# A hybrid decoder layer on one core: small fp32 products of the token mixers moved into four column strips of the TensorE array

## Chip, cores and metric

One Trainium2 chip, one NeuronCore of it. The metric is the device time of one launch in microseconds (us); the median of three runs counts. The program is one decoder layer for 2048 tokens of width 1024.

## The reference

The layer has two groups of token mixers side by side, a sandwich of RMS norms, a squared-ReLU MLP and a gated per-layer embedding. What the change touches are the two mixers and the norm of their heads:

```python
# gated DeltaNet, 4 heads, chunks of 64: a triangular solve per chunk
a_mat = eye(c) + where(strict, einsum('bhncd,bhnsd->bhncs', k_beta, k) * decay, 0)
u = triangular_solve(a_mat, v_beta, lower, unit_diagonal)
w = triangular_solve(a_mat, k_beta * exp(gc)[..., None], lower, unit_diagonal)
...
# HGRN2, 4 heads, chunks of 16: per-channel decay between query i and key j
pair = exp(where(causal, b_n[:, :, None] - b_n[:, None, :], -inf))
att  = einsum('bihd,bjhd,bijhd->bhij', q_n, k_n, pair)
...
def gated_head_norm(o, w, z):
    return o * rsqrt(mean(o * o, -1) + EPS) * w * silu(z)
```

## The kernel before, in words

Everything is kept transposed, channels on the 128 partitions and tokens along the free dimension, in four blocks of 512 tokens (q = 0 to 3). The wide products (input projection `mm`, line 1139; output projection `mmo`, lines 1022 and 1171; MLP `u` and `d` and gate `mmg`, line 1171) split each fp32 operand into two fp32r parts and add three products of 128x128 weights with 512 columns.

While the input projections run, the mixers run in between. The loop from line 1125 goes over the `works`: one for the decays (`ab`) and 32 projections for each q. Each work has 24 matmuls and is cut into three ticks of eight; after each tick `tick()` (line 376), and in its middle `half()`, step those generators that the `agenda` has for that time. A pair of heads (one GDN, one HGRN) starts every 24 ticks. `A_STEPS` (line 56) lists the ticks of the steps of `gdn_mixer`, `B_STEPS` (line 60) those of `hgrn_mixer`; the last pair has tables of its own. So two numbers in a table decide which small matmuls stand together in TensorE's queue between two wide ones. TensorE's order is the order of the code (`manual_schedule`), SyncE's too within this loop.

Three kinds of small products matter here; all are plain fp32, on the full 128x128 array.

- **HGRN's levels** (`hgrn_mixer`, `LEVELS`): the attention of a 128-token chunk is built in doubling distances s = 1, 2, 4, ..., 64. The distances 1 and 2 come from one step (line 874: four products `at_h`, 128 keys by 128 queries), 4 to 64 from one step each (line 889: two products). The result is a PSUM bank of pool `pp`, and of each 128x128 product only the entries near the diagonal are kept: VectorE's masked copy (line 896) takes them into `att`.
- **The inverse of GDN's triangular matrix** (`gdn_mixer`): 32x32 blocks are inverted on VectorE (lines 733 and 735), then two doublings join them, each by two block products: `psp`, `psx` and `pst` from 32 to 64, `psp` and `psd` from 64 to 128. The helper `pairs` (line 753) multiplies whole 128x128 operands that are mostly zero blocks, two products each.
- **The heads' norms** (`norm_steps`, line 273, called by `finish`): the sum over 128 channels is a product with a matrix of ones. The squares are split into two fp32r parts `hl` (ScalarE line 172, VectorE line 173), two products of 512 columns are added (lines 279 and 280), row 0 of the result is copied (line 282), stored, and read back as 128x4 for the square root. The norm of the early embedding tiles (`nrm_e`) uses the same function.

PSUM has eight banks: `pm` 2, `pp` 4 (also called `ph`), `po` 2. Each small product takes the next of the four `pp` banks and waits until the reader of the tile four before is done.

Of the kernel before, what the change touches and what calls it, by code (L numbers as in the profile page):

```python
# [24 lines left out]
QT = 512  # L25
NQ = T // QT
NC = QT // P
# [4 lines left out]
SB = 32  # L32
NB = P // SB
# [63 lines left out]
def trunk(ctx, tc, x, xT, pT, vecs, w_in, w_ab, gdn_a_log, gdn_dt_bias, w_out, w_up, w_down,  # L97
          w_ple, w_gate, consts, out):
    nc = tc.nc
    V, S, G, PE = nc.vector, nc.scalar, nc.gpsimd, nc.tensor  # L100
# [10 lines left out]
    ph = pp  # L111
# [8 lines left out]
    mixers = ctx.enter_context(ExitStack())  # L120
    cm = mixers.enter_context(tc.tile_pool(name="cm", bufs=1))
    cst = cm.tile([P, N_CONST, P], F32, name="cst")
    rows = cp.tile([N_ROWS, P], F32, name="rows")
# [38 lines left out]
    ones = cp.tile([P, P], F32R, name="ones")  # L162
# [7 lines left out]
    def split(t, eng, raw):  # L170

        S.activation(t[:, 0], raw, AF.Copy)  # L172
        eng.tensor_tensor(t[:, 1], raw, t[:, 0], ALU.subtract)  # L173
# [98 lines left out]

    def norm_steps(acc, scale, eps, name, done, pool=None):

        hl = st.tile([P, 2, QT], F32R, tag="hl", name=f"hl_{name}", bufs=1)
        split(hl, V, acc)
        yield
        ps = bank(f"nrm_{name}", pool or pp)
        PE.matmul(ps, ones, hl[:, 0, :], start=True, stop=False)
# [4 lines left out]
        nc.sync.dma_start(sd, row)  # L284
# [172 lines left out]
    with mixers as mctx:  # L457
# [12 lines left out]
        um = {lev: mp.tile([P, NC // 2, P], F32, name=f"um{lev}") for lev in (5, 6)}  # L470
        part = {lev: mp.tile([P, NC // 2, P], F32, name=f"part{lev}") for lev in (5, 6)}
# [148 lines left out]
        halves = [slice(0, P // 2), slice(P // 2, P)]  # L620

        def rows_of(g):
            return slice(g * SB, (g + 1) * SB)

        def gdn_mixer(q, h, live):

            n = f"g{q}_{h}"
# [8 lines left out]
            both = sm.tile([P, 2, NC], F32, tag="tail", name=f"tail_{n}")  # L636
# [93 lines left out]
            for i in range(0, SB, 2):  # L730
                j = SB - 2 - i
# [16 lines left out]
            V.transpose(flat(xt), flat(xn))  # L748
            yield

            def pairs(out, lhsT, rhs):
                for p in range(2):
                    PE.matmul(out[:, p], lhsT[:, p], rhs[:, p], start=True, stop=True)

            def two(t):
                return t.rearrange("p (n two) i -> p n (two i)", two=2)
# [3 lines left out]

            def ends(t):
                return bass.AP(t.tensor, t.offset, [list(t.ap[0]), [P, 2], [3 * SB, 2], [1, SB]])
# [5 lines left out]
            pairs(psp, um[5], ends(xn))  # L770
# [5 lines left out]
            pairs(psx, two(xt), ends(part[5]))  # L776
            pairs(pst, part[5], two(xt)[:, :, SB : 3 * SB])
# [6 lines left out]
            pairs(psp, um[6], two(xn))  # L784
# [4 lines left out]
            pairs(psd, part[6], two(xt))  # L789
# [47 lines left out]
        def hgrn_mixer(q, h, live):  # L837
# [26 lines left out]
            for lev, s in enumerate(LEVELS):  # L864
# [3 lines left out]
                m = nb // 4  # L868
                if lev == 1:
                    ps0 = bank(f"at_{n}_d", ph)[:, : QT // 2]  # L870
                    PE.matmul(ps0, one, own, start=True, stop=True)
                    ps1 = bank(f"at_{n}_{lev}", ph).rearrange("p (c n) -> p c n", c=NC)
                    for c in range(NC):
                        PE.matmul(ps1[:, c, :], k[:, blk(c)], both[:, :, c * P // 2 : (c + 1) * P // 2],
                                  start=True, stop=True)
                    chunks = ps1.rearrange("p (a b) n -> p a b n", a=2)
                    eye = bass.AP(ident.tensor, ident.offset, [list(ident.ap[0]), [1, 2], [0, 2], [2, P // 2], [1, 1]])
                    V.tensor_tensor(side_of_chunks(columns_of, 1, False),
                                    ps0.rearrange("p (a b n s) -> p a b n s", a=2, b=2, s=1), eye, ALU.mult)
                    V.tensor_tensor(side_of_chunks(columns_of, 1, True), chunks[:, :, :, : P // 2, None],  # L880
                                    mask[0][:, None, None, :, None].broadcast_to([P, 2, 2, P // 2, 1]), ALU.mult)
                    ps = chunks[:, :, :, P // 2 :]
                else:

                    ps = bank(f"at_{n}_{lev}", ph)[:, : QT // 2].rearrange("p (a b n) -> p a b n", a=2, b=2)
                    for c in range(2):
                        queries = bass.AP(qq.tensor, qq.offset + c * P + s,
                                          [list(qq.ap[0]), [QT // 2 - s, 2], [2 * s, P // (2 * s)], [1, s]])
                        PE.matmul(ps[:, :, c, :], keys[:, blk(c)], queries, start=True, stop=True)  # L889
# [229 lines left out]
        with tc.manual_schedule(engines={mybir.EngineType.SP}):  # L1119
# [32 lines left out]
            outs.close()  # L1152
            nc.sync.dma_start(*held_y.pop())

    ctx.enter_context(tc.tile_pool(name="pad", bufs=1)).tile([P, 48], F32, name="pad")
    second.append(ctx.enter_context(tc.tile_pool(name="rb", bufs=18, reuse_waits="tile")))
    f2 = ctx.enter_context(tc.tile_pool(name="f2", bufs=1, reuse_waits="tile"))
# [788 lines left out]
```

## Time and profile before

| | us |
|---|---|
| median of three runs (lowest, highest) | 2665.27 (2663.72, 2666.59) |
| the profiled execution's own time | 2665.86 |
| its span, first to last instruction | 2664.1 |
| TensorE matmul busy | 2637.0 (99%) |
| VectorE busy | 1968.0 (74%) |
| ScalarE busy | 1468.8 (55%) |
| granted TensorE clock | 1.000 |

In rows of the trace, `128*128 128x512 f32` is the rows and columns of the array that an instruction uses, then the moving operand's partitions and elements. A plain fp32 product appears as two matmul records, each with a weight load of its own, an fp32r product as one; the two records of one fp32 product are called its two passes here. PE is the matmul, PEld the weight load. The end of a matmul is modelled with the time that its result takes through the array (0.275 us for 128 moving elements, 0.389 us for 512); successive matmuls overlap in it, so what a product costs is the distance of starts: for a row of n equal passes that lasts t, (t - end of one) / (n - 1).

### The profile page before, as it was taken

To read this page: it belongs to the slowest core of one execution; us is meant where nothing else is said; L and a number is where in the kernel's file an instruction comes from. 1 tells how busy PE (TensorE), PEld (TensorE's weight loads), DVE (VectorE), ACT (ScalarE), POOL (GpSimd) and SP (SyncE) were. 2 spreads that over 40 slices of the span, in tenths; PEclk is the share of its full clock that TensorE was granted. 3 is DMA by queue.
4 is the path that set the end of the run, shared out by engine and by line. 5 is a ranking of instruction groups with operands and counts; after the bars stand their busy time and mean duration, and the time that the engine had idled before them with its cause. 6 is when DMAs were issued, how large, how long until landed. Compare 5 with 4: busy or idle time off the path is not lost.

```text
span 2664.1 us, 38284 instructions
## 1 busy us (share of the span) xinstructions
PE 2637.0 (99%) x12745; PEld 2209.8 (83%) x12745; DVE 1968.0 (74%) x4029; ACT 1468.8 (55%) x2991; POOL 136.4 (5%) x147
## 2 busy tenths in 40 slices
PE   8999999999999999999999999999999999999999
PEld 6888888888888888877888888888888888888887
DVE  7778777786677677578988867767877765468775
ACT  6666555465455456566565555555554555565431
POOL 0000000000000000010000000001000001101000
PEclk9999999999999999999999999999999999999999
DMA  8787777667666775682766476666544465677663
GB/s 281 274 261 256 241 268 238 227 225 240 218 212 221 234 220 176 203 250 102 242 213 202 164 242 219 213 204 207 199 171 145 160 236 187 198 253 250 209 224 124
DMA packets 267766, 573.51 MB, mean 215 GB/s; under 512 B 55578, under 2 KB 60152, under 8 KB 250416
## 3 DMA queue, kind: packets, MB, share of 16 engines
q1 hardware_dynamic: 265264, 566.86, 63.9%
q0 software_dynamic: 2304, 4.20, 0.9%
q8 instruction: 101, 1.65, 0.3%
q14 instruction: 97, 0.79, 0.1%
HBM read 410.57 MB, written 160.37 MB: 214 GB/s over the span
## 4 chain that ended last, share of the span: by engine, by line
PE 60%; DMA 3%; DVE 2%; ACT 1%; issue 1%; SPq 0%; POOL 0%; DVEq 0%; ACTq 0%; POOLq 0%
PE d L1171 23%; PE u L1171 23%; PE mmg L1171 7%; PE mm L1139 3%; PE mmo L1022 1%; PE mme L199 1%; DMA mixT<-mixd 1%; DMA yod<-yo 1%; DMA yo<-in_xT_dram 0%; DVE t L173 0%; DVE acc_o L242 0%; DMA sys_g<-ud_g 0%; DMA wd<-in_w_down_dram 0%; PE at_h L889 0%; DMA ud_g<-u_g 0%
## 5 line engine op out<-in xcount | busy, mean ns | idle before, releaser
L1139 PE MATMUL mm<-xt,w 128*128 128x512 f32 x3072 | 783.6, 400 | 1.3 <-DVE w L173 0.8
L1139 PEld LDWEIGHTS mm<-xt,w 128*128 128x128 f32 x3072 | 553.3, 189 | 102.0 <-issue 1.3
L1171 PE MATMUL d<-db,da 128*128 128x512 f32 x2688 | 612.8, 389 | 0.0
L1171 PEld LDWEIGHTS d<-db,da 128*128 128x128 f32 x2688 | 504.5, 188 | 104.8
L1171 PE MATMUL u<-t,wu 128*128 128x512 f32 x2604 | 591.2, 389 | 0.0
L1171 PEld LDWEIGHTS u<-t,wu 128*128 128x128 f32 x2604 | 488.7, 188 | 101.5
L226 DVE TENSOR_TENSOR db<-db 128x512 fp32r<-128x512 f32 x224 | 159.3, 711 | 58.5 <-ACT db L225 57.9
L1569 DVE TENSOR_TENSOR u<-u,u 128x512 f32<-128x512 f32 x224 | 150.1, 681 | 51.3 <-PE u L1171 49.7
L225 ACT ACTIVATE db<-db 128x512 fp32r<-128x512 f32 x224 | 141.0, 629 | 65.6 <-DMA db<-hid 60.4
L1171 PE MATMUL mmg<-h2T,wg 128*128 128x512 f32 (+1 forms) x792 | 174.7, 383 | 0.0
L1171 PEld LDWEIGHTS mmg<-h2T,wg 128*128 128x128 f32 x792 | 145.5, 188 | 29.1
L1612 ACT ACTIVATE u<-u 128x512 f32<-128x512 f32 x128 | 80.8, 631 | 152.3 <-DVE u L1569 151.6
L173 DVE TENSOR_TENSOR da<-da 128x512 fp32r<-128x512 f32 x128 | 95.4, 745 | 88.8 <-ACT da L172 85.5
L172 ACT ACTIVATE da<-da 128x512 fp32r<-128x512 f32 x128 | 80.5, 629 | 126.1 <-DMA da<-sumd 106.5
L1171 PE MATMUL mmo<-mixT,w_out 128*128 128x512 f32 x600 | 138.4, 390 | 1.5 <-DVE w_out L173 1.1
L1171 PEld LDWEIGHTS mmo<-mixT,w_out 128*128 128x128 f32 x600 | 112.2, 188 | 26.6 <-DVE w_out L173 2.3
L172 ACT ACTIVATE wu<-a 128x512 fp32r<-128x512 f32 x124 | 75.1, 624 | 54.6 <-DMA a<-in_w_up_dram 52.7
L173 DVE TENSOR_TENSOR wu<-a,wu 128x512 fp32r<-128x512 f32 x124 | 85.8, 694 | 9.3 <-ACT wu L172 9.1
L173 DVE TENSOR_TENSOR da<-dr,da 128x512 fp32r<-128x512 f32 x96 | 68.2, 710 | 22.9 <-ACT da L172 21.4
L1613 ACT ACTIVATE u<-u 128x512 f32<-128x512 f32 x128 | 80.4, 628 | 3.0
L172 ACT ACTIVATE da<-dr 128x512 fp32r<-128x512 f32 x96 | 60.5, 631 | 30.5 <-DMA dr<-in_w_down_dram 19.6
L242 POOL TENSOR_TENSOR acc_y<-acc_y,sq_y 128x512 f32<-128x512 f32 x28 | 37.9, 1355 | 757.8 <-ACT sq_y L241 757.8
(391 smaller groups left out, 3810.8 us busy)
## 6 DMA issues: line engine op xcount, KB each, us to landing
w<-cache_in SPq DMA_DIRECT2D x96, 1024.0 KB
db<-hid SPq DMA_DIRECT2D x224, 256.0 KB
cache_in<-w SPq DMA_DIRECT2D x32, 1024.0 KB
hid<-u SPq DMA_DIRECT2D x128, 256.0 KB
da<-sumd SPq DMA_DIRECT2D x128, 256.0 KB
a<-in_w_up_dram SPq DMA_DIRECT2D x124, 256.0 KB
hid<-ht SPq DMA_DIRECT2D x96, 256.0 KB
dr<-in_w_down_dram SPq DMA_DIRECT2D x96, 256.0 KB
```

The source lines that it names most:

```text
L172: S.activation(t[:, 0], raw, AF.Copy)
L173: eng.tensor_tensor(t[:, 1], raw, t[:, 0], ALU.subtract)
L199: PE.matmul(ps, a, b, start=i == 0, stop=i == n - 1)
L225: S.activation(t[:, 0], plain(t), AF.Copy)
L226: V.tensor_tensor(t[:, 1], plain(t), t[:, 0], ALU.subtract)
L242: eng.tensor_tensor(acc, acc, sq, ALU.add)
L1022: PE.matmul(ps, w[:, term // 2, k, :], xin[q][k][:, term % 2, :], start=i == 0, stop=i == 3 * KD - 1)
L1139: PE.matmul(ps, *terms[i], start=i == 0, stop=i == nt - 1)
L1171: PE.matmul(ps, a, b, start=start, stop=stop)
L1569: V.tensor_tensor(c[new], c[old], ps, ALU.add)
L1612: S.activation(c[k], c[k], AF.Relu)
L1613: S.activation(c[k], c[k], AF.Square)
```

## The change

1. `strip(g, out, lhsT, rhs)` issues a product on a 128x32 part of the array: column strip g takes 32 of the stationary's columns and writes partitions 32g to 32g+31. Levels of distance 1 to 32 become four strips per product, each with the 32 keys of its strip and only the queries near them: 32 moving columns instead of 128. The last level (64) stays on the full array.
2. The inverse's products become strips too, each multiplying only the block that is needed: 32 moving columns for `psp5`, `pst5`, `psx5`, 64 for `psp6` and `psd6`.
3. The norm of 512 tokens becomes four strips, one for each 128 tokens, in plain fp32 with 32 columns of ones. The split `hl` is gone; ScalarE copies a 128x128 tile instead of a 1x512 row, and the store takes four rows of 128.
4. The levels' results lie in one PSUM bank of their own, `at_all`, zeroed once; levels 4 and up use its halves in turn. For that `pp` has three banks while the mixers run, and four again afterwards (pool `pq`).
5. GDN's norm steps come one tick later, HGRN's four, and so the copies and stores that follow them.

```diff
-           + (53, 55, 57, 59, 60, 61, 63, 64))
+           + (53, 56, 58, 60, 61, 62, 64, 65))
-B_STEPS = (24, 26, 28, 30, 32, 34, 36, 38, 40, 42, 44, 45, 46, 48, 50, 52, 53, 54, 56, 57)
+B_STEPS = (24, 26, 28, 30, 32, 34, 36, 38, 40, 42, 44, 45, 46, 52, 54, 56, 57, 58, 60, 61)
...
-    pp = ctx.enter_context(tc.tile_pool(name="pp", bufs=4, space=PSUM))
+    pp = mixers.enter_context(tc.tile_pool(name="pp", bufs=3, space=PSUM))
+    at_all = mixers.enter_context(tc.tile_pool(name="pa", bufs=1, space=PSUM)).tile([P, QT], F32, name="at_all")
+    V.memset(at_all, 0.0)
...
-        hl = st.tile([P, 2, QT], F32R, tag="hl", name=f"hl_{name}", bufs=1)
-        split(hl, V, acc)
         yield
-        ps = bank(f"nrm_{name}", pool or pp)
-        PE.matmul(ps, ones, hl[:, 0, :], start=True, stop=False)
-        PE.matmul(ps, ones, hl[:, 1, :], start=False, stop=True)
-        row = acc[0:1, :]
-        S.activation(row, ps[0:1, :], AF.Copy)
+        ps = bank(f"nrm_{name}", pool or pp)[:, :P]
+        for c in range(NC):
+            PE.matmul(ps[c * SB : (c + 1) * SB, :], ones.bitcast(F32)[:, :SB], acc[:, blk(c)], start=True, stop=True,
+                      tile_position=(0, c * SB))
+        S.activation(acc[:, :P], ps, AF.Copy)
...
+        def strip(g, out, lhsT, rhs):
+            PE.matmul(out, lhsT, rhs, start=True, stop=True, tile_position=(0, g * SB))
...
-            def pairs(out, lhsT, rhs):
+            def in_halves(out, lhsT, rhs, other):
                 for p in range(2):
-                    PE.matmul(out[:, p], lhsT[:, p], rhs[:, p], start=True, stop=True)
+                    for g in range(NB):
+                        to = halves[g // 2 ^ other]
+                        strip(g, out[rows_of(g), p, to], lhsT[:, p, rows_of(g)], rhs[:, p, to])
...
-                    for c in range(NC):
-                        PE.matmul(ps1[:, c, :], k[:, blk(c)], both[:, :, c * P // 2 : (c + 1) * P // 2],
-                                  start=True, stop=True)
+                    for c in range(NC):
+                        for j in range(NB):
+                            strip(j, ps1[rows_of(j), c].rearrange("p (l n) -> p l n", l=2)[:, :, near[j]],
+                                  k[:, c * P + j * SB : c * P + (j + 1) * SB],
+                                  both[:, :, c * P // 2 : (c + 1) * P // 2][:, :, near[j]])
```

TensorE's queue around the first step of a GDN inverse's second product, before: the norm of the previous GDN head stands in a tick of its own, with the transposes of the next keys, and the block products and a level stand one tick later. Names: `nrm_g` is the norm, `t_kg` the transposes, `psx_g` and `pst_g` the inverse, `at_h` the level, `mm` the wide products.

```order
L279 MATMUL nrm_g_0_2013<-hl_g_0_1957,ones 128x512
L280 MATMUL nrm_g_0_2013<-hl_g_0_1957,ones 128x512
L595 MATMUL t_kg_2_2022<-cst,y_kg_2_1888 128x128 x4
L1139 MATMUL mm_0_2_1977<-xt_5_538,w_0_2_1808 128x512 x2
L1139 MATMUL mm_0_2_1977<-xt_6_554,w_0_2_1808 128x512 x3
L1139 MATMUL mm_0_2_1977<-xt_7_557,w_0_2_1808 128x512 x3
L753 MATMUL psx_g_1_2050<-part_577,xt_g_1_1873 128x64 x2
L753 MATMUL pst_g_1_2051<-xt_g_1_1873,part_577 128x64 x2
L889 MATMUL at_h_1_3_2062<-qk_h_1_1553,keys_h_1_2_1999 128x2x64 x2
```

The same place in the changed kernel: the rows with 32 partitions first are strips.

```order
L595 MATMUL t_kg_2_2087<-cst,y_kg_2_1936 128x128 x4
L1165 MATMUL mm_0_2_2037<-xt_5_543,w_0_2_1864 128x512 x2
L1165 MATMUL mm_0_2_2037<-xt_6_559,w_0_2_1864 128x512 x3
L1165 MATMUL mm_0_2_2037<-xt_7_562,w_0_2_1864 128x512 x3
L280 MATMUL nrm_g_0_2114<-osq_g_0_2018,ones 32x128 x4
L627 MATMUL pst_g_1_2125<-xt_g_1_1921,part_582 32x32 x4
L627 MATMUL psx_g_1_2124<-part_582,xt_g_1_1921 32x32 x2
L627 MATMUL pst_g_1_2125<-xt_g_1_1921,part_582 32x32 x4
L627 MATMUL psx_g_1_2124<-part_582,xt_g_1_1921 32x32 x2
L627 MATMUL at_all<-qk_h_1_1612,keys_h_1_2_2070 32x2x16 x8
```

The norm has moved behind the wide products, so that 24 strips stand in one uninterrupted group where six full-array products stood, and the transposes `t_kg` keep their place. In the whole program the strips form 95 such groups.

The other place is the first level of an HGRN head on TensorE, in the changed kernel: the norm of the previous HGRN head `nrm_h` has moved four ticks down and stands right ahead of the first level's 16 strips; the full-array product `at_h_1_d`, which stood ahead of the level, comes after.

```order
L816 MATMUL psb_g_0_3_1957<-r_g_0_3_1919,xt_full 128x128
L1165 MATMUL mm_0_2_1944<-xt_4_527,w_0_2_1787 128x512 x3
L1165 MATMUL mm_0_2_1944<-xt_5_543,w_0_2_1787 128x512
L280 MATMUL nrm_h_0_1965<-osq_h_0_1834,ones 32x128 x4
L627 MATMUL at_all<-hb_h_1_1887,qk_h_1_1612 32x2x16 x16
L889 MATMUL at_h_1_d<-att_h_1_1886,one 128x256
L1165 MATMUL mm_0_2_1944<-xt_5_543,w_0_2_1787 128x512 x2
```

Here 20 strips stand in one group between two full-array stretches. The program has 1,488 strips in place of 352 fp32 products and 72 fp32r products.

More of the change, by code (lines that the diff above doesn't have):

```diff
@@ L273, in norm_steps @@
     def norm_steps(acc, scale, eps, name, done, pool=None):
[L275 to L276 removed]
         yield
[L278 to L282 removed]
+        ps = bank(f"nrm_{name}", pool or pp)[:, :P]
[3 more added lines that the diff above has]
+        S.activation(acc[:, :P], ps, AF.Copy)
         sd = dr.tile([1, QT], F32, name=f"sd_{name}")
[L284 removed]
+        nc.sync.dma_start(sd.rearrange("o (c n) -> (o c) n", n=P), acc[::SB, :P])
         yield
@@ L769, in gdn_mixer @@
             psp = half_bank("psp5")
-            pairs(psp, um[5], ends(xn))
+            for p in range(2):
+                for g in range(NB):
+                    strip(g, psp[rows_of(g), p, rows_of(1 - g % 2)], um[5][:, p, rows_of(g)],
+                          two(xn)[:, p, rows_of(0 if g % 2 else NB - 1)])
             for g in range(NB):
@@ L775, in gdn_mixer @@
             psx, pst = half_bank("psx5"), half_bank("pst5")
-            pairs(psx, two(xt), ends(part[5]))
-            pairs(pst, part[5], two(xt)[:, :, SB : 3 * SB])
+            for p in range(2):
+                for g in range(NB):
+                    strip(g, pst[rows_of(g), p, rows_of(g % 2)], part[5][:, p, rows_of(g)],
+                          two(xt)[:, p, rows_of(1 + g % 2)])
+                for g in (1, 2):
+                    strip(g, psx[rows_of(g), p, rows_of(g - 1)], two(xt)[:, p, rows_of(g)],
+                          part[5][:, p, rows_of(0 if g == 1 else NB - 1)])
             for g, to in ((1, 0), (2, 1)):
@@ L783, in gdn_mixer @@
             psp = pair_bank("psp6")
-            pairs(psp, um[6], two(xn))
+            in_halves(psp, um[6], two(xn), 1)
             for a in range(2):
@@ L788, in gdn_mixer @@
             psd = pair_bank("psd6")
-            pairs(psd, part[6], two(xt))
+            in_halves(psd, part[6], two(xt), 0)
             xf = by_pair(xt_full)
@@ L883, in hgrn_mixer @@
                 else:
-                    ps = bank(f"at_{n}_{lev}", ph)[:, : QT // 2].rearrange("p (a b n) -> p a b n", a=2, b=2)
+                    ps = at_all[:, lev % 2 * QT // 2 : (lev % 2 + 1) * QT // 2].rearrange("p (a b n) -> p a b n", a=2, b=2)
                     for c in range(2):
-                        queries = bass.AP(qq.tensor, qq.offset + c * P + s,
-                                          [list(qq.ap[0]), [QT // 2 - s, 2], [2 * s, P // (2 * s)], [1, s]])
-                        PE.matmul(ps[:, :, c, :], keys[:, blk(c)], queries, start=True, stop=True)
+                        start = qq.offset + c * P + s
+                        if 2 * s == P:
+                            queries = bass.AP(qq.tensor, start, [list(qq.ap[0]), [QT // 2 - s, 2], [1, s]])
+                            PE.matmul(ps[:, :, c, :], keys[:, blk(c)], queries, start=True, stop=True)
+                            continue
+                        for j in range(NB):
+                            out = ps[rows_of(j), :, c, near[j]]
+                            if s < SB:
+                                queries = bass.AP(qq.tensor, start + j * SB, [
+                                    list(qq.ap[0]), [QT // 2 - s, 2], [2 * s, SB // (2 * s)], [1, s]])
+                            else:
+                                out = ps[rows_of(j), j % 2, c, rows_of(j // 2)]
+                                queries = bass.AP(qq.tensor, start + j % 2 * (QT // 2 - s) + j // 2 * 2 * s,
+                                                  [list(qq.ap[0]), [1, s]])
+                            strip(j, out, keys[:, c * P + j * SB : c * P + (j + 1) * SB], queries)
                 late, early = (side(g, nb, 1, x).broadcast_to([P, 2, m, s]) for x in (True, False))
```

8 lines of the change are left out of this document (4 added, 4 removed).

## The prediction

> **What bounds the kernel now.** I read the page's busy times first, then the windows for the stretch in which the mixers run, then the waits of TensorE in it.
>
> ```profile
> PE 2637.0 (99%) x12745; PEld 2209.8 (83%) x12745; DVE 1968.0 (74%) x4029; ACT 1468.8 (55%) x2991; POOL 136.4 (5%) x147
> 45.00:1075.00 1030.00, 1023.15 (x5622) 879.01 (x5622) 761.39 (x2158) 592.46 (x1531) 58.62 (x73) 1.00 0.71 234
> PE kk_g L683 <- ACT y_qg L574: 2.5, 3, 1.8
> PE psc_g L810 <- ACT w_g L807: 1.1, 2, 0.7
> ```
>
> The second row is the mixers' window: of 1030 us TensorE is busy 1023, VectorE 761, ScalarE 592, at clock 1.00. The two last rows are the largest of the eight waits of TensorE in that window; all eight add up to 6.8 us. So TensorE's queue sets the time: whatever the change takes from it or adds to it moves the end, and relief of other engines brings at most those few microseconds. Two instructions of 0.63 and 0.68 us per head go with the norm's split:
>
> ```profile
> L173 DVE TENSOR_TENSOR hl_g<-osq_g,hl_g 128x512 fp32r<-128x512 f32 x16 | 10.9, 682 | 0.1
> L172 ACT ACTIVATE hl_g<-osq_g 128x512 fp32r<-128x512 f32 x16 | 10.1, 631 | 5.6 <-DVE osq_g L610 5.3
> ```
>
> They lie beside the wide products on engines with over 25% idle; I count them as nothing. If VectorE became the bound, they would be worth their sum, about 0.7 us a head.
>
> **What is taken away.** These groups are the products replaced (one x counts one pass), followed by rows from the order of time that give the distance between passes.
>
> ```profile
> L874 PE MATMUL at_h<-hb_h,qk_h 128*128 128x128 f32 x128 | 16.9, 275 | 0.0
> L889 PE MATMUL at_h<-qk_h,keys_h 128*128 128x128 f32 x320 | 50.8, 281 | 0.7 <-DVE acc_vg L566 0.7
> L753 PE MATMUL pst_g<-xt_g,part 128*128 128x64 f32 x64 | 9.8, 275 | 0.0
> L753 PE MATMUL psp_g<-xn_g,um 128*128 128x128 f32 x64 | 9.7, 274 | 0.0
> L753 PE MATMUL psx_g<-part,xt_g 128*128 128x64 f32 x64 | 8.9, 261 | 0.0
> L279 PE MATMUL nrm_g<-hl_g,ones 128*128 128x512 f32 x16 | 6.4, 401 | 0.0
> 107.01 1.05 PE L874 MATMUL at_h<-hb_h,qk_h 128*128 128x128 f32 x8
> 431.86 0.56 PE L753 MATMUL psx_g<-part,xt_g 128*128 128x64 f32 x4
> 432.25 0.61 PE L753 MATMUL pst_g<-xt_g,part 128*128 128x64 f32 x4
> 58.69 0.84 PE L1139 MATMUL mm<-xt,w 128*128 128x512 f32 x3
> ```
>
> Eight passes in 1.05 us with an end of 0.275 stand (1.05 - 0.275) / 7 = 0.111 us apart; I use 0.112. Four passes of `pst` with only 64 elements stand (0.61 - 0.275) / 3 = 0.112 apart: a pass of 64 elements costs as much as one of 128, so there the weight load of 128 columns sets the pace. Only the first pass of such a group, whose weights came in behind a wide product, is shorter: `psx` has its four in 432.25 - 431.86 = 0.39, that is 0.06 + 3 x 0.11. Wide products stand (0.84 - 0.389) / 2 = 0.226, say 0.227, apart.
>
> Levels: 128 passes of L874 and 256 of the 320 of L889 (the last level stays), 384 x 0.112 = 43.0 us. The inverse: five groups of 64 passes, 320 x 0.112 = 35.8, less 32 first passes that are 0.055 shorter, 34.0. Norms: two products for each of 36 norms, 72 x 0.227 = 16.3. Together **93.3 us**, 3.5% of the kernel; more can't be saved.
>
> **What is added: the strips.** There are 1,488 strips, two passes each if fp32 goes on as now: 2,176 passes with 32 moving elements, 512 with 64, 288 with 128. No row shows a pass of 32 columns. From the rows above, load and stream of 128 each take about 0.107, so a quarter is an estimated 0.027. But a floor on issue speaks in these rows, a weight load and the matmul behind it:
>
> ```profile
> 59.65 0.14 PEld L542 LDWEIGHTS ps_gb<-cst,gbb 36*128 36x128 f32 x1
> 59.68 0.23 PE L542 MATMUL ps_gb<-cst,gbb 36*128 36x36 f32 x1
> 107.79 0.54 PEld L1139 LDWEIGHTS mm<-xt,w 128*128 128x128 f32 x3
> 107.82 0.94 PE L1139 MATMUL mm<-xt,w 128*128 128x512 f32 x3
> ```
>
> Both times the matmul starts 0.03 us after its load, however busy the array still is. I take 0.031 as the least distance of two passes. The upper end is the distance of the four small `ps_gb` passes, 0.062 (four starts from 59.47 to 59.68, below). Whether neighbouring strips run at the same time no row shows. If TensorE takes passes in order, the second pass of a strip must wait for the first, which uses the same columns, while the first pass of the next strip can run beside it: two at a time at best. Then a pass costs half its stream or 0.031, whichever is more: 0.031 at 32 and 64 elements (half of 0.06 is less), 0.056 at 128. Sum: 2,176 x 0.031 = 67.5, 512 x 0.031 = 15.9, 288 x 0.056 = 16.1, together 99.5 us. **The strips as such give back 93.3 and cost 99.5: +6.2 us.** The reason is the number of passes, 776 before and 2,976 after: the work per pass falls to a quarter, but the count rises nearly fourfold.
>
> **What is added: changes of the array's shape.** The trace has such a change already: the four transposes `ps_gb` use 36 rows of the array, between wide products on 128.
>
> ```profile
> 59.47 0.25 PE L542 MATMUL ps_gb<-cst,gb 36*128 36x36 f32 x1
> 59.83 0.97 PE L1139 MATMUL mm<-xt,w 128*128 128x512 f32 x3
> 59.46 0.14 PEld L542 LDWEIGHTS ps_gb<-cst,gb 36*128 36x128 f32 x1 [0.35 <-issue]
> 59.83 0.76 PEld L1139 LDWEIGHTS mm<-xt,w 128*128 128x128 f32 x4
> PEld ps_gb L542 <- issue: 1.1, 4, 0.4
> ```
>
> The third wide product of the row that began at 58.69 starts at 59.14 (58.69 + 0.84 - 0.39). In a run of equal shapes the next weights come in right behind that start. Here the load waits until 59.46, when the product has streamed (0.227) and its results have left; PEld is idle 0.35 with nothing that the profile shows, four times out of four (last row: 1.1 us). On the way back the load waits from 59.68 to 59.83, and isn't hidden: the row of three ends at 60.80, so its third product starts at 60.41 and the first in truth at 59.95. From 59.14 to 59.95 are 0.81 us for one wide product and four small ones, 0.227 + 4 x 0.062 = 0.475: 0.33 us lost to one group of another shape. A strip's load is shorter by an estimated 0.03, so I take 0.30. With 95 groups that is **+28.5 us**. The ends: nothing, if columns change without emptying the array, and 95 x 0.33 = 31.4.
>
> The Trainium skill, page "TensorEngine Tiling (Array Packing)", section "Key Properties", says that a change of tiling mode drains TensorE; the 0.33 us above agree, and by the opposite rule the sum would be 28.5 us lower.
>
> **The rest.** The norms' four ticks put stores of `mixd` back by some 8 us; they are read after the mixers, and the last pair keeps its own table, so nothing waits. `pp` has three banks instead of four, but the levels no longer take from it. The tightest reuse I find is `pst` after the transposes `t_kg`, whose last reader is this:
>
> ```profile
> 431.26 1.12 ACT L661 ACTIVATE kt_g<-t_kg,tail_g 128x128 f32<-128x128 f32 x4
> ```
>
> It ends at 432.38; `psx` started at 431.86, but in the changed order `pst` comes after a shape change and a norm, near 432.5. If it waits, the wide products behind it wait too: 0 to 0.5 us in 12 to 16 pairs, 0 to 8 us. With `at_all`, the step after the first level must wait for the masked copy:
>
> ```profile
> L896 DVE COPY_PREDICATED att_h<-cst,at_h x96: 414/440/743, 108.9 to 1064.3; 128x256 f32<-128x256 uint32 x96
> L889 PEld LDWEIGHTS at_h<-qk_h,keys_h x320: 186/192/192, 111.3 to 1063.5; 128*128 128x128 f32 x160
> ```
>
> In the first head the copy ends by 109.7 and the next level's weights start at 111.3; 1.6 us of margin. I take 1 us for both. A single extra fill of a bank costs nothing beside the start.
>
> **Sum.** 6.2 + 28.5 + 1 = +35.7 us against the profiled execution's own 2665.86, which is 0.6 above the median: **2701 us**, 1.3% slower.
>
> **The rivals.** (a) *Four strips at once, faster.* If the passes of four strips overlap fully, each four costs two passes of one: 272 fours x 2 x 0.031 = 16.9, 64 x 2 x 0.06 = 7.7, 36 x 2 x 0.112 = 8.1, together 32.7 us. Then 32.7 - 93.3 + 28.5 = -32: 2634 us. It decides for faster once the mean pass is below (93.3 - 28.5) / 2,976 = 0.022 us. Against it speak the order of the passes and the 0.03 at issue; for it, that four small groups use separate columns. Chance 0.18.
>
> The Trainium skill, "TensorE: Matmul & The Clock Gate", section "Part 3: Packing small matmuls — row/col tiling", has concurrent tiles start about 4 ns apart and three column strips of 512 gain 2.38 times. By that rule the time would come out near (a) for single passes; no row here shows it.
>
> (b) *Two at a time without a floor at issue.* A strip costs one stream: 1,088 x 0.031 + 256 x 0.06 + 144 x 0.112 = 65.2, plus 0.03 at each group's end, 68 us; 68 - 93.3 + 28.5 = +3: 2669, within what can be told from no change. Chance 0.17. (c) *No two strips together*, so that the change doesn't do what strips are for: 67.5 + 512 x 0.06 + 288 x 0.112 = 130.5; +37.2 + 28.5 = 2732 us. For it speaks that the loads in this trace come one ahead of the matmul and no more. Chance 0.21. (d) *0.062 per pass*, as `ps_gb` has it: 2,176 and 512 x 0.062 are 166.7, the norms' 288 x 0.112 another 32.3, together 199.0; +105.7 + 28.5: 2800. The `ps_gb` passes load 128 columns, which explains their 0.062 as well; chance 0.09.
>
> **How the numbers follow.** The forecast has 0.35. The range leaves out (d) and the lower side of (a): 2635 to 2745, which takes in (b), (c) and the unknown waits. A measurement of this kernel can tell about 0.2%, 5 us, from no change. Faster: (a) and a third of (b) with cheap shape changes, 0.25. Within 0.2%: another third of (b) and a little, 0.09. Slower: the rest, 0.66.
>
> **What would show it.** The start-to-start distance inside a group of strips: 0.031 for the forecast, 0.01 to 0.016 for (a) and (b), 0.06 for (d); the norm's eight passes in about 0.5 us for the forecast, 0.22 for (a), 0.9 for (c). PEld idle by issue ahead of each of 95 groups and behind it: 0.3 us for the pair, or my largest term is wrong. TensorE should wait for `pp` readers less than 8 us. Beyond the mixers' end, near 1075 us, every stage should keep its length; if they don't, something else has moved.

## The result and the profile after

| | before | after |
|---|---|---|
| median of 4 runs each | 2665.93 us | 2688.96 us (2682.16 to 2691.28) |
| ratio | | 1.0083, interval 1.0063 to 1.0103 |
| profiled execution, span | 2665.86, 2664.1 | 2687.49, 2685.5 |

The change makes the kernel 0.83% slower, some 22 us. The forecast was 2701 in a range of 2635 to 2745. One execution is left out of all that follows: the profiled one of a kernel among the experiments took 9309 us, its other three 2652 to 2654, so that kernel has no row of a trace.

The profile of the changed kernel, its row for the window of the mixers, then that of the last 1364 us, beside the last 1364 us of the kernel before (columns: window, its length, busy times of TensorE, its weight loads, VectorE, ScalarE and GpSimd, granted clock, DMA share, GB/s):

```profile
45.00:1075.00 1030.00, 992.01 (x7661) 812.11 (x7660) 733.63 (x2101) 552.61 (x1477) 59.22 (x77) 0.99 0.69 232
```

```profile
1321.20:2685.20 1364.00, 1359.89 (x6033) 1126.38 (x6032) 998.50 (x1541) 701.39 (x1168) 57.99 (x44) 1.00 0.61 202
```

```profile
1300.00:2664.00 1364.00, 1359.65 (x6022) 1126.63 (x6020) 999.35 (x1543) 703.40 (x1170) 58.05 (x44) 1.00 0.60 202
```

Behind the mixers nothing has moved: the two last rows lie 21.2 us apart in start, and the busy times of TensorE, VectorE and ScalarE agree within 0.3%. All of the change is in the mixers, and there two things happened at once. TensorE is busy for 992.0 of 1030 us instead of 1023.2: its idle time went from 6.8 to 38.0 us, and its clock shows 0.99. The queue of TensorE, which was the bound, now has holes.

**A balance by stretches.** Between two wide products, whose starts are 0.227 us apart when nothing stands between them, I take the time that a group of small products adds, counted up to the second wide product behind it, because the first one's start is recorded early; groups with the same small products form a kind. The shortest of each kind is the price of the products themselves; what the others take above their shortest is waiting. A third column has what wide products take above 0.227 between themselves. From 40 to 1110 us of each trace, against the kernel before (the 72 wide products of its norms, 16.3 us, counted with the small ones where they went):

| kernel | small products | waits in groups | wide ones | sum | span against before |
|---|---|---|---|---|---|
| changed kernel | -30.2 | +41.7 | +9.6 | +21.1 | +21.4 |
| strips with the old tables | -23.3 | +7.7 | +5.3 | -10.3 | -10.4 |
| changed kernel, row load later | -27.2 | +16.8 | +4.6 | -5.8 | -6.8 |

So the strips, with all changes of shape, *gave* 30 us, and 51 us came in elsewhere; 13 of these 51 remain with the old tables, 38 came with the new ones. The first and third rows price the same products at 30.2 and 27.2, so the split is good to some 3 us. The group of `psp5` and a level, for one, fell from 0.905 to 0.591 us.

**What a strip costs.** In the order of time of TensorE in the changed kernel stand two lone groups, a level and a norm, each between wide products:

```profile
109.22 2.68 PE L1165 MATMUL mm<-xt,w 128*128 128x512 f32 x11
111.83 0.33 PE L627 MATMUL at_all<-qk_h,keys_h 128*32 128x32 f32 x16
112.09 2.12 PE L1165 MATMUL mm<-xt,w 128*128 128x512 f32 x8
...
367.12 1.16 PE L1165 MATMUL mm<-xt,w 128*128 128x512 f32 x4
368.21 0.43 PE L280 MATMUL nrm_h<-osq_h,ones 128*32 128x128 f32 x8
368.57 1.19 PE L1165 MATMUL mm<-xt,w 128*128 128x512 f32 x4
```

The level has 16 passes (eight strips, two passes each) in 0.33 us, an end of 0.197 included: 0.13 / 15 = 0.009 us from start to start. Single records show how: the four strips' first passes start 6 to 7 ns apart, then the four second passes, and a strip's next pass comes 32 ns after its last. Four strips at a time, then, and 0.032 per strip: rival (a). From the last wide start ahead (109.22 + 2.68 - 0.389 = 111.51) to the second one behind (112.09 + 2.12 - 0.389 - 6 x 0.227 = 112.46) are 0.95 us; less 0.454 and the 4 x 0.032 of the passes leaves 0.37 for entering and leaving the shape. For the norm the same sum is 0.57 - 2 x 0.112 = 0.35. By the single records of the trace, up to the second wide product behind, both come to 0.33. The shape change is what the forecast took from `ps_gb`. Its entering shows as PEld idle behind "issue", 9.2 / 26 = 0.35 us each:

```profile
PEld psp_g L627 <- issue: 9.2, 26, 0.4
```

**Who waits.** The waits of TensorE in the mixers' window (45 to 1075 us) of the changed kernel, the largest:

```profile
PE psa_g L811 <- DVE S_g L823: 11.3, 7, 3.6
PE psc_g L821 <- ACT w_g L818: 8.9, 9, 3.2
```

The largest are not at strips at all but in GDN's recurrence (`psa`, `psb`, `psc`), which waits for VectorE and ScalarE. Those engines are less busy than before; they wait themselves. VectorE's waits for transfers in the same window, changed kernel, then before:

```profile
DVE pr_g L721 <- DMA sys_g<-ud_g: 34.4, 15, 5.5
...
DVE og_g L616 <- DMA rsb_g<-rd_g: 27.1, 14, 4.5
...
DVE og_h L616 <- DMA rsb_h<-rd_h: 20.1, 13, 2.7
```

```profile
DVE og_g L616 <- DMA rsb_g<-rd_g: 16.0, 11, 3.7
...
DVE pr_g L717 <- DMA sys_g<-ud_g: 13.2, 11, 2.8
...
DVE og_h L616 <- DMA rsb_h<-rd_h: 9.1, 7, 3.5
```

81.6 against 38.3 us. `rsb` is the spread row of the late norms; `sys` is the next head's matrix, which feeds the inverse on VectorE. The order of SyncE's queue shows what joins them: first before, near 190 us, then the changed kernel at the same place in the program.

```profile
188.96 0.32 SPq L293 DMA_DIRECT2D rd_g<-m_g  x1
189.33 1.85 SPq L696 DMA_DIRECT2D ud_g<-u_g  x4
192.78 0.34 SPq L253 DMA_DIRECT2D rsb_g<-rd_g  x1
193.57 0.53 SPq L705 DMA_DIRECT2D sys_g<-ud_g  x1
```

```profile
191.60 3.08 SPq L700 DMA_DIRECT2D ud_g<-u_g  x4
194.78 0.56 SPq L293 DMA_DIRECT2D rd_g<-m_g  x1
196.26 0.34 SPq L618 DMA_DIRECT2D mixd<-og_h  x1
201.01 0.32 SPq L255 DMA_DIRECT2D rsb_g<-rd_g  x1
201.51 0.58 SPq L709 DMA_DIRECT2D sys_g<-ud_g  x1
```

Before, `rd_g` goes ahead of `ud_g`, and `sys_g` follows the end of `ud_g`'s issue (191.18) by 2.4 us. After, `rd_g` goes behind `ud_g`, SyncE stands at `rsb_g` until `rd_g` has landed, and `sys_g` comes 6.8 us behind the end of `ud_g`'s issue (194.68). But `rsb_g` holds `sys_g` for 0.7 of these 6.8 us only: by the landing records of the trace (the semaphore updates of each transfer), `ud_g` itself has landed 6.1 us behind its issue (2.3 before). Over the 16 heads `ud_g` takes 84.7 us from the end of its issue to its landing, against 67.3 before, and `sys_g` goes out 13.7 us behind these landings, against 1.7. So `sys` is late in two ways: it stands behind `rsb_g`, and `ud_g`, for which it waits, lands later. Why `ud_g` lands later is open.

The second path is VectorE's own order. The chain of what ended last in the changed kernel, at 647 us:

```profile
647.44 7.40 DMA rd_g<-m_g
...
654.86 6.09 DMA rsb_g<-rd_g
...
660.97 0.75 DVE og_g L616
661.72 0.27 DVE r_g L813
...
662.13 0.46 PE psb_g L816 x2
```

The 2 KB of `rd_g` take 7.40 us from issue to landing, the row load 6.09, then `og_g` runs on VectorE, and `r_g`, for which TensorE's `psb` waits, only behind it.

**A clock that falls.** One wait leaves a tail. Changed kernel, TensorE in the order of time, and the windows ahead of and at these rows (the number ahead of the DMA share is the granted clock):

```profile
210.75 1.17 PE L1165 MATMUL mm<-xt,w 128*128 128x512 f32 x4
...
216.98 0.64 PE L821 MATMUL psc_g<-w_g,kt_g 128*128 128x128 f32 x2 [3.24 <-ACT w_g L818]
...
218.13 2.05 PE L1165 MATMUL mm<-xt,w 128*128 128x512 f32 x4
```

```profile
214.00:218.00 4.00, 1.02 (x5) 1.02 (x6) 3.61 (x11) 3.97 (x10) 0.00 (x0) 0.90 0.80 197
218.00:220.20 2.20, 2.20 (x9) 1.81 (x8) 1.78 (x6) 1.83 (x4) 0.00 (x0) 0.50 1.05 438
```

Four wide products take 2.05 us instead of 1.17, at clock 0.50, behind a wait of 3.24 us. That occurs three times in the mixers, for 3 to 10 wide products each, behind waits of 3.24, 2.79 and 3.60 us. The Trainium skill, "TensorE: Matmul & The Clock Gate", section "Part 1: The HAM clock gate (the "warmup" mystery)", halves the clock after an idle window of about 3.4 us; these rows agree on the half, and show that less idle time is enough.

The length of the wait alone doesn't decide: one of 2.84 us, from 417.16 to 420.00, left the clock at 1.00. The clock records of the trace have the three drops at 217.18, 288.86 and 548.27 us, which are 21 and 76 times 3.413 us apart. In the 3.41 us that end at a drop TensorE was idle for 3.2, 2.4 and 2.4 us; the wait of 2.84 us lies across two such stretches, with 1.4 us of idle time in each. In the other traces, too, the drops in the mixers lie on a grid of 3.413 us, and the least idle time ahead of one was 1.7 us, the most without a drop 1.9. So here about half of such a stretch is enough.

### The profile page after: what moved, and what is told of

It reads as the page before. It is cut to its first block, busy times and chain, and to the rows that moved or that the text cites. A ratio compares the mean times of both kernels' runs of the same rounds, so it can differ in the third digit from the quotient of the medians.

```text
span 2685.5 us, 42572 instructions
## 1 busy us (share of the span) xinstructions
PE 2625.1 (98%) x14945; PEld 2156.9 (80%) x14945; DVE 1949.0 (73%) x3994; ACT 1433.7 (53%) x2955; POOL 137.1 (5%) x147
## 4 chain that ended last, share of the span: by engine, by line
PE 63%; DMA 5%; DVE 4%; issue 2%; ACT 1%; SPq 1%; POOL 0%; DVEq 0%; POOLq 0%; ACTq 0%
PE d L1198 23%; PE u L1198 22%; PE mm L1165 7%; PE mmg L1198 6%; DMA rd_g<-m_g 1%; PE mmo L1048 1%; PE mme L201 1%; DMA gf_g<-gd 1%; DMA sys_g<-ud_g 0%; DMA rsb_g<-rd_g 0%; DMA mixT<-mixd 0%; DVE xs_g L739 0%; DVE pr_g L737 0%; DMA yo<-in_xT_dram 0%; DMA w<-cache_in 0%
## 5 line engine op out<-in xcount | busy, mean ns | idle before, releaser
L1198 PEld LDWEIGHTS mmo<-mixT,w_out 128*128 128x128 f32 x600 | 112.2, 188 | 28.5 <-DVE w_out L175 2.5
```

Of the source, the lines that this page charges most:

```text
L1198: PE.matmul(ps, a, b, start=start, stop=stop)
```

## The experiments

Three theories for the 51 us were on trial at first: **L**, the later norms disturb a queue; **T**, groups of strips are shorter, so that ticks are shorter and the chains between them no longer fit, whatever the tables; **B**, three banks in `pp` are too few. Each batch ran beside the kernel before on one chip; the ratio is to that. "idle" is 1030 us less the busy time of TensorE in the window 45 to 1075, "rsb + sys" VectorE's waits for the transfers `rsb_g`, `rsb_h` and `sys_g` there.

| kernel | median us | ratio, interval | idle | rsb + sys |
|---|---|---|---|---|
| before | | 1 | 6.8 | 38.3 |
| changed kernel | 2688.96 | 1.0083, 1.0063 to 1.0103 | 38.0 | 81.6 |
| strips, old tables | 2659.45 | 0.9971, 0.9958 to 0.9983 | 15.4 | 48.9 |
| new tables, no strips | 2693.83 | 1.0097, 1.0082 to 1.0112 | 26.5 | 61.9 |
| three banks only | 2672.31 | 1.0019, 1.0009 to 1.0029 | 8.5 | 41.1 |
| strips without the norms', old tables | 2653.79 | 0.9943, 0.9926 to 0.9959 | | |
| HGRN's ticks alone | 2670.25 | 1.0011, 1.0001 to 1.0020 | 27.1 | 69.2 |
| GDN's ticks alone | 2672.18 | 1.0021, 1.0011 to 1.0031 | 21.8 | 49.9 |
| norms on GpSimd's queue | 2780.91 | 1.0422, 1.0407 to 1.0438 | 84.1 | 92.5 |
| no norm strips, one bank for two | 2658.25 | 0.9958, 0.9944 to 0.9972 | 17.4 | 46.5 |
| strip by strip | 2665.63 | 0.9988, 0.9977 to 0.9999 | 14.3 | 42.7 |
| row load later | 2663.07 | 0.9973, 0.9963 to 0.9984 | 20.6 | 42.0 |
| HGRN's norm ten ticks later | 2682.02 | 1.0053, 1.0035 to 1.0071 | 39.6 | 68.6 |
| no norm strips, row load later | 2658.35 | 0.9956, 0.9943 to 0.9970 | 17.2 | 44.2 |

**Strips with the old tables.** The changed kernel, but

```diff
-           + (53, 56, 58, 60, 61, 62, 64, 65))
+           + (53, 55, 57, 59, 60, 61, 63, 64))
-B_STEPS = (..., 46, 52, 54, 56, 57, 58, 60, 61)
+B_STEPS = (..., 46, 48, 50, 52, 53, 54, 56, 57)
```

> The changed kernel with the two step tables of before: all strips stay, the norms go back to their old ticks, 114 groups of strips instead of 95. Three theories on where the changed kernel loses about 50 us in waits of TensorE, while its strips themselves gain about 30. Theory L (late norms: the norm's stores and loads now stand in SyncE's queue ahead of the inverse's and the weights' transfers): waits of TensorE in the mixers fall to under 15 us and the time is 2640 to 2650 us. Theory T (shorter ticks: TensorE needs less time per tick, and chains of DMA, VectorE and ScalarE no longer fit, whatever the table): waits stay above 30 us and the time is 2680 to 2700. Theory B (three PSUM banks instead of four): as T, 2680 to 2700, with TensorE waiting for readers of PSUM tiles.

0.9971: faster than before, and 30 us faster than the changed kernel though it has 19 groups more. T falls; L's direction holds, 10 us above its range. The norms now stand alone in a group of 0.557 us where their two full products took 0.454.

**The new tables alone**, in the kernel before, without a strip:

> The kernel before with only the two step tables of the change: no strip, four banks. Theory L: TensorE's waits in the mixers rise from 7 to 35 us or more and the time is 2695 to 2720 us. Theory T: the ticks keep their length, so 2661 to 2672. Theory B: 2661 to 2672.

1.0097, +26 us: L's direction, just under its 2695, with 26.5 us of idle time where it had 35. The largest waits are those of the same two products as in the changed kernel (the kernel before with the new tables, TensorE, 45 to 1075 us):

```profile
PE psc_g L810 <- ACT w_g L807: 8.8, 7, 2.1
PE psa_g L800 <- DVE S_g L812: 8.8, 7, 2.2
```

The loss belongs to the tables and needs no strips.

**Three banks alone**, in the kernel before: `pp` with three banks during the mixers.

```diff
-    pp = ctx.enter_context(tc.tile_pool(name="pp", bufs=4, space=PSUM))
+    pp = mixers.enter_context(tc.tile_pool(name="pp", bufs=3, space=PSUM))
...
```

> The kernel before with three banks in pool pp while the mixers run (the fourth is set aside, zeroed, and not used). Theory B: 2685 to 2715 us. Theories L and T: 2663 to 2672, a few us at most where the block products follow the key transposes.

1.0019, 2 to 8 us: the three banks cost something, and far less than the 20 to 50 us that B had.

**Strips for the levels and the inverse alone**, norms as before on the full array, both old tables:

> Strips for the levels and the inverse only; norms as before (two fp32r products of 512 columns on the full array), old tables, three banks; 82 groups of strips. Theory L: the strips' gain shows, 2638 to 2650 us, within 6 us of the run with strips for the norms too, since a lone norm in strips costs about as much as one on the full array. Theories T and B: 2680 to 2700.

0.9943, the lowest ratio of all kernels here, with 82 groups; by the intervals it can't be told from two of those below (0.9956 and 0.9958). It is 4 us above L's range. Taking the norms out of the strips is worth some 7 us against the first experiment, with intervals that overlap a little. The lone groups explain a part: a norm in strips adds 0.557 us there, on the full array 0.454.

**Which table.** HGRN's four ticks alone, then GDN's one tick alone, each in the changed kernel:

> The changed kernel with HGRN's new ticks alone: GDN's table is the old one, all strips stay. 102 groups of strips instead of 95 (after) or 114 (strips with both old tables). If the late norms' small transfers, which stand in SyncE's queue ahead of the inverse's and the weights' transfers, cost the time, then the four ticks of HGRN are the larger part: 2675 to 2690 us. Rival, that only both moves together collide (norms g and h then issue at nearly one place): at most 2662, since the groups saved are worth 12 x 0.3.

> The changed kernel with GDN's new ticks alone (one tick later); HGRN's table is the old one, all strips stay; 107 groups. If the late norms cost the time by how late they are, one tick costs little: 2656 to 2668 us, and the two single moves add up to the changed kernel's 2689 within 6 us. Rival, that GDN's one tick is what breaks the order (its norm passes the next head's inverse in SyncE's queue): 2675 or more.

1.0011 and 1.0021. Against the strips with old tables that is +11 and +13 us. Both miss what was expected: HGRN's four ticks cost 5 us less than the low end, GDN's one tick 4 more than the high end. They add up (2659 + 11 + 13 = 2683, by ratios, against 2689), so no collision of both is needed. But the price is not in proportion to the lateness: one tick costs as much as four. What counts, I think, is what the move passes: GDN's one tick puts `rd_g` behind `ud_g` and `rsb_g` into the tick of `sys_g`. The landing records show that much. Over the 16 heads, with GDN's tick alone, `sys_g` goes out 13.2 us behind the landings of `ud_g` (1.9 for the strips with old tables), and `ud_g` lands as before (67.1 us, 66.5). With HGRN's ticks alone `sys_g` stands behind them for 3.1 us in all, and it is `ud_g` that lands later, 78.8 us. But the path from there to TensorE isn't shown for GDN's tick: VectorE's "rsb + sys" is 49.9 us against 48.9, and SyncE's waits for `rd` (45 to 1100 us) 57.6 against 55.9.

**Another queue for the norms' transfers.** In the changed kernel, GpSimd instead of SyncE issues the four small transfers of each head; in short:

```diff
-        nc.sync.dma_start(...)   # sd, m, rd, rsb
+        nc.gpsimd.dma_start(...)
```

> The changed kernel with both new tables and all strips, but the four small transfers of each head's norm (store of the sums, load, store of the roots, load of the spread row) are issued by GpSimd instead of SyncE. If SyncE's order is the path by which the late norms delay the rest, TensorE's waits fall and the time goes back to 2655 to 2670 us. Rival, that the norms' buffers (og, osq, the result bank) are held longer, whatever the queue: 2683 to 2695. GpSimd's own price to issue a transfer, seen in no row, could hide a part: 2670 to 2680 would leave it between.

1.0422: neither. GpSimd takes its work in order too, and it now stands at the norm's store; behind that stand the clearing of `xn` and the power of `m`. Waits of GpSimd and of TensorE in this kernel (45 to 1100 us), then VectorE's (45 to 1075):

```profile
POOL sd_h L284 <- ACT osq_h L282: 493.4, 13, 46.0
```

```profile
PE psp_g L627 <- DVE xn_g L790: 23.2, 6, 7.9
```

```profile
DVE og_g L616 <- DMA rsb_g<-rd_g: 43.0, 12, 7.1
DVE og_h L616 <- DMA rsb_h<-rd_h: 41.6, 10, 8.8
...
DVE pr_g L721 <- DMA sys_g<-ud_g: 7.9, 3, 3.7
```

As a test it fails, since it makes a larger wait than it removes. One row is of some use: with SyncE free of the norms, `sys` is waited for 7.9 us instead of 34.4. That speaks for a part of L, that `sys` was late because of what stood ahead of it in SyncE's queue; but this kernel takes 92 us more, which gives each transfer more time as well.

**The row load later.** The changed kernel with both new tables and all strips; only `rsb`, its reader `og` and the store behind come *still later*, by two ticks:

```diff
-           + (53, 56, 58, 60, 61, 62, 64, 65))
+           + (53, 56, 58, 60, 61, 64, 66, 67))
-B_STEPS = (..., 52, 54, 56, 57, 58, 60, 61)
+B_STEPS = (..., 52, 54, 56, 57, 60, 62, 63)
```

> The changed kernel with both new tables and all strips; only the load of the spread row (rsb) and the steps behind it come later still, GDN's by 2 ticks and HGRN's by 2. In the changed kernel GDN's rsb load stands in the tick of the next head's load sys and waits in SyncE's queue for rd to land; here sys goes ahead of it. If SyncE's order is the path, the waits of VectorE for sys fall from 34 us to below 22, SyncE's for rd from 104 to below 40, and the time falls though the norms end later: 2660 to 2675 us. Rival, that the norms' lateness itself costs (buffers held): 2690 to 2705.

0.9973: of the 30 us that the tables cost, 29 come back by the ratios, by being later. SyncE at the same place as above, and VectorE's waits:

```profile
192.16 3.18 SPq L700 DMA_DIRECT2D ud_g<-u_g  x4
195.44 0.38 SPq L293 DMA_DIRECT2D rd_g<-m_g  x1
200.07 0.58 SPq L709 DMA_DIRECT2D sys_g<-ud_g  x1
...
202.28 0.60 SPq L255 DMA_DIRECT2D rsb_g<-rd_g  x1
```

```profile
DVE pr_g L721 <- DMA sys_g<-ud_g: 25.7, 14, 3.3
...
DVE og_h L616 <- DMA rsb_h<-rd_h: 12.3, 8, 2.7
...
DVE og_g L616 <- DMA rsb_g<-rd_g: 4.0, 4, 2.0
```

`sys_g` now goes ahead of `rsb_g`. At this place it still comes 4.7 us behind the end of `ud_g`'s issue, all of it the landing of `ud_g`; over the 16 heads the landings of `ud_g` take 60.8 us in all, and `sys_g` goes out 1.5 us behind them. SyncE's waits for `rd` (45 to 1100 us) fall from 104.2 to 18.9. VectorE's waits for `sys` stayed above the 22 that I expected; those for `rsb` fell from 47 to 16. That lateness as such explains the 30 us is refuted. But the edit relieves two queues at once, SyncE's at `rsb` and VectorE's at `og`; a run with `og` alone later would tell them apart, and there is none.

**HGRN's norm ten ticks later.** Here `rsb_h` goes behind the next `sys`, and GDN has its old table:

> All strips, GDN's old table, and HGRN's norm not 4 but 10 ticks later (its rsb load 12 ticks after the old place, behind the next head's ud store and sys load instead of just ahead of them). 103 groups. If the place in SyncE's queue counts, this is not slower than the 4 ticks alone (2670) and may be faster: 2660 to 2668 us, with VectorE's waits for sys below 25 us. Rival, that lateness itself costs, in proportion: 11 us per 4 ticks give 2685 to 2690.

1.0053, slower, and 3 us under the rival's range. Getting behind `sys` isn't enough: `rsb_h` comes one tick after `rd_h`, as in the other tables, and SyncE still stands there (this kernel, 45 to 1100 us):

```profile
SPq L255 <- DMA rd_h<-m_h: 49.9, 12, 6.7
```

SyncE's wait for `xd`, the inverse's next transfer, is 69.1 us (21.5 before); but it is 50.5 in the changed kernel and 54.5 with the row load later, where little was lost. Over the 16 heads `sys_g` goes out 2.2 us behind `ud_g`'s landings, and these take 67.5 us, much as with the old tables; so what stands ahead of `sys` isn't the loss here. VectorE still waits 32.1 us for `sys`, not the 25 or less that I expected: `sys_g` itself takes 103.4 us to land, against 87.2 for the strips with old tables. Whether the standing queue or the lateness costs can't be told from this run.

**Strip by strip.** Strips for the levels and the inverse alone; each group issues all products of one strip before those of the next:

```diff
-                    for c in range(NC):
-                        for j in range(NB):
+                    for j in range(NB):
+                        for c in range(NC):
                             strip(j, ...)
```

> The same strips in the levels and the inverse alone (norms on the full array, both old tables, 82 groups; that kernel took 0.9943 of the before, about 2654 us), but each group issues all products of one strip before those of the next, so that neighbours in the queue share columns. The count of passes is the same. If four strips overlap only because neighbouring products go to different strips and TensorE takes its queue in order, a group of 8 passes or more grows from about 0.07 us per four strips towards 4 times that: the first level (32 passes) by 0.7 to 1.2 us, each other group by 0.2 to 0.4, over ten groups a head 3 to 5 us, 16 heads 45 to 80 us: 2700 to 2735. Rival, that each strip has a queue of its own and order doesn't count: 2652 to 2658.

0.9988, between the two expectations and nearer to the rival: 8 to 12 us more than the same strips in turn (0.9958 and 0.9943), not 45 to 80. The first level's 32 passes in the kernel with strips in turn (the one with one bank for two), then strip by strip:

```profile
105.95 0.46 PE L629 MATMUL at_all<-hb_h,qk_h 128*32 128x32 f32 x32
```

```profile
106.63 0.90 PE L629 MATMUL at_all<-hb_h,qk_h 128*32 128x32 f32 x32
```

Less an end of 0.196 these are 0.26 and 0.70 us: 8.5 and 22.7 ns a pass. In the second, passes follow each other 32 ns apart within a strip. The four longest records (217 ns against 196, which I take for each strip's first) start 0.153 us apart. That is five passes, not eight, so the last three of a strip run beside the first of the next. A strip is free again after 0.032 us, then, and order counts, but strips still overlap in part. My expectation took a strip's price times four for every group; most groups are eight strips, and there the order costs much less (the group with `psp6`: 2.508 us against 2.473).

**One bank for `psx` and `pst`**, with strips for the levels and the inverse alone:

> Strips for the levels and the inverse alone, norms on the full array as before, both old tables (82 groups of strips), and the inverse's two products psx and pst share one bank instead of taking one each, so that the three banks of the pool go round later. If three banks cost the 5 us that the kernel before with three banks showed, and pst's bank is where: 2647 to 2651 us. If that price sits elsewhere: 2652 to 2655, as the same kernel without the shared bank.

0.9958 against 0.9943, intervals overlapping: no gain, and 3 us above even the second expectation. The 5 us of three banks lie elsewhere; where, is open.

**The best kernel with the row load later:**

> Strips for the levels and the inverse alone, norms on the full array at their old ticks (that kernel took 0.9943 of the before), and the load of the spread row with the steps behind it 2 ticks later for both mixers, as in the run that took the changed kernel back to 0.9973. If SyncE's standing still for rd costs time in the old tables too (58.7 us of such waits in the before): SyncE's waits for rd fall below 20 us and the ratio to 0.990 to 0.993, 2641 to 2650 us. If in the old tables these waits stand where nobody needs the queue: 0.993 to 0.996, no change from the kernel without the later load.

0.9956: the second expectation. SyncE's waits for `rd` fell to 6.2 us (58.7 before), and the time didn't. So in the old tables they stand where nobody needs the queue. A wait in a queue has no price of its own; what stands behind it has.

## Why the prediction was right in sign and wrong in its steps

- **What is taken away**, 93.3 us: right as far as the sum shows. With shape changes of 95 x 0.33 = 31.4 the strips themselves cost 93.3 - 30.2 - 31.4 = 31.7 us, near rival (a)'s 32.7.
- **The step that failed first**: "the first pass of the next strip can run beside it: two at a time at best". It runs four at a time. The 0.031 that I took as a floor on any two passes is the distance within one strip, 0.032; across strips it is 0.006 to 0.007. 99.5 us forecast, some 32 measured, 68 us too many. The Trainium skill, "TensorE: Matmul & The Clock Gate", section "Part 3: Packing small matmuls — row/col tiling", has concurrent tiles start about 4 ns apart; the runs show 6 to 7 ns, and side with it against my order of passes.
- **Shape changes**, 28.5 us from 0.30 each: right within 3 us, 0.33 in the lone groups. The starts around one `ps_gb` were enough. The idle time of PEld was misread: the last row says 1.1 us for four, 0.35 once and about 0.25 three times. Nor do the rows give 0.107 for load and stream of 128 columns, but 0.11. Neither enters the sum.
- **The step that failed second**: "The norms' four ticks put stores of `mixd` back ... so nothing waits", with the banks 1 us in all. I followed the last transfer of the moved step and not its others: `rd`, `rsb` and `sd` are also issued later, into a queue that serves in order, and `og` stands in VectorE's queue. 51 us came in where 1 was forecast, 38 of them with the new tables; net of the 19 groups that they save, the tables cost 30 us with strips and 26 without.
- **Banks**: 0 to 8 us, 1 taken; 2 to 8 measured alone.
- **The end of the mixers**: every stage behind kept its length, as foretold.
- The two failed steps have opposite signs, -68 and +50, so the sum of 2701 missed by 12 only. That is luck. Rival (a) had the strips right and not the time: even with the old tables they stood at 2659, 25 us above its 2634, with 13 us of waits and 19 groups more. That "TensorE waits for `pp` readers less than 8 us" held told nothing on the waits that came.

What is shown: strips gain, the tables lose, and a later row load gives the loss back. What is argued from the rows, not separated: how much of it goes through SyncE's queue to `sys`, how much through later landings, and how much through VectorE's queue to `r_g`.

## What to carry to other kernels

When a step is moved by a tick, list each transfer that it issues and look up, for each in-order queue, what it now passes and what stands behind the place where the queue waits for a landing: one tick cost as much here as four. A store and the load that reads it back want distance in the queue, not just order; here two more ticks between them were worth 29 us with the new tables, and nothing with the old ones. Small products in column strips are worth it where several share one change of shape: a lone norm lost 0.1 us by it, a level shared with the inverse gained 0.3.

## What the runs showed of the hardware

- Four column strips start passes 6 to 7 ns apart, a strip takes its next pass after 32 ns (32 columns, up to 32 moving elements), and the order in the queue counts: 8.5 ns a pass in turn, 22.7 strip by strip.
- A change of the array's shape and back cost 0.33 us by the single records, for a lone level and a lone norm in strips; for the 36-row transposes the prediction has the same 0.33.
- The granted clock fell to 0.50 behind waits of 2.79, 3.24 and 3.60 us and not behind one of 2.84, and 3 to 10 wide products took nearly twice their time. The drops lie on a grid of 3.413 us, at the end of stretches in which TensorE was idle for 2.4 us or more.
- The 2 KB of `rd_g` took 3.02 us from issue to landing in a step of the chain of before (at 879.74 us) and 7.40 in the chain after; the transfer had not grown.
